# One set of weight buffers for two phases of a two-layer encoder, and the second phase's first inputs in the first phase's list schedule

## The chip, the cores and the metric

The kernel runs on one core of a Trainium2 chip. The core has five instruction queues that run side by side and meet at semaphores: TensorE (PE, matrix multiplication, with its weight loads shown as PEld), VectorE (DVE), ScalarE (ACT), GpSimd (POOL) and SyncE (SP), which here issues every DMA. The metric is device time in microseconds for one launch; smaller is better.

## What is computed

The reference is a trunk of two layers on 512 positions with 1024 channels (batch 1). Layer 0 mixes with a recurrent part (RWKV-7, both directions) and a long convolution (Hyena, by Fourier transform); layer 1 mixes with neighbourhood attention. Each layer then has a gated feed-forward part with a width-3 convolution, and a gated embedding.

```python
for i in range(DEPTH):                       # DEPTH = 2
    if i % 2 == 0:
        z = rmsnorm(h, mix_norm[j]) @ mix_w_in[j]
        y_a = rwkv7_bidir(z[..., :RWKV_COLS], ...)     # a scan in time, per head a 64 x 64 state
        y_b = hyena_bidir(z[..., RWKV_COLS:], ...)     # irfft(rfft(s) * rfft(kernel))
        h = h + jnp.concatenate([y_a, y_b], axis=-1) @ mix_w_out[j]
    else:
        z = rmsnorm(h, na_norm[j]) @ na_w_qkv[j]
        h = h + neighbourhood_attention(z, ...) @ na_w_out[j]
    h = h + conv_ffn(h, ffn_norm[i], ffn_w_up[i], ffn_conv_w[i], ffn_conv_b[i], ffn_w_down[i])
    h = h + per_layer_embedding(h, p[i], ple_norm[i], ple_w_gate[i], ple_w_proj[i])
```

## The kernel before

Activations lie channel-major: `self.h` is eight tiles of 128 channels x 512 positions. Every float32 product is made of three matmuls on parts of reduced precision: an operand x is split into a high part `xh` and the rest `xl`, a weight into `whi` and `wlo` (or two `wp` tiles), and `mm3` (line 647) adds xh·whi, xh·wlo and xl·whi in PSUM. So each weight costs a load, a cast (high part, on ACT) and a subtraction (rest).

**First phase: layer 0's mixer, `mixer0` (line 783).** Its instructions are not issued as they are written. A `Plan` (line 227) records them as steps, `both_mixers` (line 924) gives each piece of work a group (`part`, line 917), and `schedule` (line 408) makes a list schedule: at each point the engine that can start first takes the ready step with the highest rank. A rank is 1000 times the group's number from the table `ORDER` (line 830), or from `MOVED` where that names the group, plus the step's longest path to the end (`ranks`, line 393). With `DRAG` 0 (line 233) every step of a group has at least the rank of the group's first step. `in_order` (line 852) then holds each engine to this order.

The groups: `x` and `norm` load and split the input; `low`, `z` 0 to 3 and `hyena` 0 to 3 project it with `mix_w_in`, one 128-column block after another (`columns`, line 1036: 24 matmuls of 128x512); `prep` makes the recurrent part's operands for each pair of heads and direction; `inverse` inverts the triangular blocks of pair m (a long chain of short DVE instructions and small matmuls); `scan` m (line 1372) goes through 8 chunks in time, each with three steps in which PE waits for ACT or DVE (tiles `uv`, `r0`, `dg`, `x`); `out` m finishes the pair. `filters`, `fparts`, `kf`, `signals`, `ab`, `back` are the convolution by Fourier tables (`in_dft_f`, `in_dft_i`); `emb` 0 and 1 multiply the layers' embeddings by `proj` and store the result to DRAM (`pj_d`). `early`, `mid` and `last` are the output projection of the two halves of h, in three sets of inputs (`mix_w_out_a`, `mix_w_out_b`); `last` needs the last pair's output.

Weights of this phase are taken by `item` (line 882) in halves of 512 columns: a raw tile from `wr` (3 buffers), two split tiles from `wp` (12 buffers); the cast is ACT's, the subtraction POOL's. Parts that are kept longer go to slabs (`sl`, 39 buffers), the phase's common tiles.

**Second phase.** With the first phase's pools closed, `run` (line 744) opens `wraw`, `whi`, `wlo` (3 buffers of 1024 columns each), and the rest is issued as written: `ffn(0)`, `ple(0)`, `mixer1`, `ffn(1)`, `ple(1)`. `ffn` (line 1656) begins with `norm` (line 693): eight splits of h into `xh`, `xl` scaled by the gain, eight squares on ACT, seven additions on POOL. `gemm` (line 661) then goes through the up-weights in chunks of two input tiles (24 matmuls) and makes the row sums of the squares (`sums`) as a matmul after the second chunk.

Of the kernel before, what the change touches and what calls it, by code (L numbers as in the profile page):

```python
# [19 lines left out]
P = 128  # L20
# [206 lines left out]
class Plan:  # L227
# [5 lines left out]
    DRAG, SMALL = 0.0, 3  # L233
# [359 lines left out]
class Kern:  # L593
# [67 lines left out]
    def gemm(self, wname, g, k0, k1, xs, evac, then=(), rounds=1):  # L661
# [10 lines left out]
        for kc in range(k0, k1, KC):  # L672
# [3 lines left out]
            chunks.append((kc, nk, *self.load_split(src, nk * W)))  # L676
# [16 lines left out]
    def norm(self, h, gain):  # L693
# [44 lines left out]
    def gemm_pools(self, st, bufs, side):  # L738
        self.wraw = self.pool(st, "wraw", bufs=bufs, side="right")
        self.whi = self.pool(st, "whi", bufs=bufs, side=side)  # L740
        self.wlo = self.pool(st, "wlo", bufs=bufs, side=side)


    def run(self):
        nc, a = self.nc, self.a
        with ExitStack() as top:
# [19 lines left out]
            with ExitStack() as st:  # L766
                self.gemm_pools(st, 3, "left")
# [15 lines left out]
    def mixer0(self):  # L783
# [16 lines left out]
        with ExitStack() as st:  # L800
# [6 lines left out]
            self.rstd0 = self.h[4]  # L807
# [6 lines left out]
            self.wr = self.pool(st, "wr", bufs=3, side="right")  # L814
            self.wp = self.pool(st, "wp", bufs=self.PARTS, side="right")
# [12 lines left out]
    SLABS, PARTS = 39, 12  # L828

    ORDER = dict(start=180, x=200, low=198.5, norm=120, filters=75, scan=100, inverse=84, prep=80, z=79, out=60,  # L830
                 hyena=50, fparts=40, kf=67, signals=70, ab=58, back=46, early=30, emb=25, consts=86, mid=72,
                 last=99, norm1=98, next=55)


    MOVED = {("back", 0): 57.5, ("back", 2): 35.5, ("early", 0): 28.5, ("hyena", 2): 26.5, ("kf", 0, 1): 30.5,
             ("mid", 1): 32.5, ("scan", 0): 86.5, ("early", 1): 36.5}

    def order(self, group):
# [7 lines left out]
        if name in ("prep", "z"):  # L846
            n = [5 * n[0]]
# [34 lines left out]
    def item(self, held=False):  # L882

        t = []
        srcs = self.sources.popleft()
        for y in srcs:
            t.append(self.wr.tile([P, S], F32, name="wr"))
            self.nc.sync.dma_start(out=t[-1], in_=y)
        r = [self.slab(F32R) if held else self.wp.tile([P, S], F32R, name="wp") for _ in range(2)]
        self.nc.scalar.copy(r[0], t[0])  # L890
        if len(t) == 1:
            self.tt(r[1], t[0], r[0].bitcast(F32), ALU.subtract, self.nc.gpsimd)
        else:
            self.nc.gpsimd.tensor_copy(out=r[1], in_=t[1])
        return r

    def weights(self, name, g):
# [6 lines left out]
        for k in range(0, K // P, KC):  # L904
            nk = min(KC, K // P - k)
            src = self.a[name][base + k * P * W:base + (k + nk) * P * W].rearrange("(p a) -> p a", p=P)
            out += [(src[:, i:i + 512],) for i in range(0, nk * W, 512)]
        return out

    def table(self, name, fc, j):  # L910
        src = self.a[name][fc]
        return src[:, j * 1024:j * 1024 + 512], src[:, j * 1024 + 512:j * 1024 + 1024]
# [4 lines left out]
    def part(self, group, what, *args, sources=()):  # L917

        before, self.nc.group = self.nc.group, group
        self.sources = deque(sources) if sources else self.sources  # L920
# [3 lines left out]
    def both_mixers(self):  # L924
# [3 lines left out]
        self.sources = deque()  # L928
# [44 lines left out]
        where = (self.h[0:2], self.h[2:4], self.h[5:7], (self.h[7], self.slab()))  # L973
# [19 lines left out]
        for l in range(2):  # L993
            for g in range(2):
                for j in range(4):
                    what = [(a["pT"][l, k],) for k in range(2)] if (g, j) == (0, 0) else []
# [950 lines left out]
```

## Time and profile before

| | us |
|---|---|
| median of 3 runs | 1597.08 (1593.35 to 1598.9) |
| the profiled execution | 1602.47 |
| its span | 1600.7 |
| PE busy | 1531.0 (96%) |
| DVE busy | 973.9 (61%) |
| ACT busy | 718.8 (45%) |
| POOL busy | 341.0 (21%) |
| mean granted clock of TensorE | 0.974 |

The profile is of one execution. Busy time is the time in which an engine had an instruction running; idle time before an instruction is put down to what ended it (its releaser). Matmuls overlap, so their pace is the distance from start to start. The granted clock is a share of full speed: 1.00 is 2.4 GHz, 0.50 is 1.2 GHz, and a value between is a stretch with both.

### The profile page before, as it was taken

The page shows a single profiled execution, that of the slowest core. Times are in us where ns is not written, and L with a number is a line of the kernel's source. Part 1 is how long each engine was busy: PE and PEld are TensorE (multiplying, and loading weights), DVE is VectorE, ACT ScalarE, POOL GpSimd, SP SyncE. Part 2 cuts the span into 40 slices and gives each one's busy share as a digit, 9 for nine tenths or more (in the row PEclk, how much of TensorE's full clock was granted, in tenths as well). Part 3 has the DMA queues.
Part 4 walks back from the last instruction along what each step waited for, and adds up shares of the span by engine and source line. Part 5 has one row for each costly group of instructions (what it writes and reads, how often), then busy time and mean ns, then how long its engine had stood idle before and what let it go on. Part 6 is the DMA issues. An engine that isn't in the chain of part 4 may idle for free.

```text
span 1600.7 us, 24569 instructions
## 1 busy us (share of the span) xinstructions
PE 1531.0 (96%) x9520; PEld 1219.6 (76%) x9520; DVE 973.9 (61%) x1618; ACT 718.8 (45%) x1210; POOL 341.0 (21%) x296
## 2 busy tenths in 40 slices
PE   7999999979797999999999999999999999999998
PEld 6766777657585888888888878777678888888886
DVE  4875677775654477534674664565666665366655
ACT  5636455535344344313443554564554443144332
POOL 4654554433554000000001332011030000000020
PEclk9999999979898999999999999999999999999999
DMA  7456464766354323223243234224122332222431
GB/s 235 122 126 193 139 195 130 226 206 203 128 184 135 100 96 102 92 96 102 92 128 122 86 112 124 94 81 130 61 66 79 105 105 93 93 88 97 160 104 66
DMA packets 114583, 195.97 MB, mean 122 GB/s; under 512 B 27537, under 2 KB 57105, under 8 KB 114466
## 3 DMA queue, kind: packets, MB, share of 16 engines
q1 hardware_dynamic: 114466, 194.40, 38.4%
q8 instruction: 75, 1.23, 0.3%
q14 instruction: 42, 0.34, 0.1%
HBM read 163.95 MB, written 28.84 MB: 120 GB/s over the span
## 4 chain that ended last, share of the span: by engine, by line
PE 84%; DVE 5%; DMA 4%; ACT 3%; SPq 2%; issue 1%; POOL 1%; POOLq 0%; DVEq 0%; ACTq 0%
PE g L627 61%; PE b L590 19%; DVE w L590 3%; SPq L590 2%; PE m L627 2%; PE s L627 1%; ACT w L590 1%; PE m L1892 1%; DMA wr<-in_mix_w_in 1%; POOL w L590 1%; DMA wr<-in_dft_f 0%; POOL nacc L633 0%; ACT oh L641 0%; DVE u L633 0%; DVE uv L590 0%
## 5 line engine op out<-in xcount | busy, mean ns | idle before, releaser
L633 DVE TENSOR_TENSOR wlo<-wraw,whi 128x1024 fp32r<-128x1024 f32 x180 | 227.8, 1267 | 322.5 <-ACT whi L641 317.7
L641 ACT CAST whi<-wraw 128x1024 fp32r<-128x1024 f32 x180 | 188.2, 1046 | 406.7 <-PE g L627 398.5
L627 PE MATMUL g<-xh,whi 128*128 128x512 f32 x832 | 326.8, 393 | 8.9 <-ACT whi L641 8.9
L627 PE MATMUL g<-xh,wlo 128*128 128x512 f32 x832 | 325.3, 391 | 1.0 <-DVE wlo L633 1.0
L627 PE MATMUL g<-xl,whi 128*128 128x512 f32 x832 | 324.9, 391 | 0.0
L627 PEld LDWEIGHTS g<-xh,whi 128*128 128x128 f32 x832 | 157.0, 189 | 43.0 <-ACT whi L641 9.3
L627 PEld LDWEIGHTS g<-xh,wlo 128*128 128x128 f32 x832 | 156.8, 188 | 34.7 <-DVE wlo L633 1.7
L627 PEld LDWEIGHTS g<-xl,whi 128*128 128x128 f32 x832 | 157.1, 189 | 32.3
L633 POOL TENSOR_TENSOR nacc<-nsq 128x512 f32<-128x512 f32 x5 | 8.8, 1767 | 760.5 <-PE g L627 639.6
L590 PE MATMUL b<-xh,wp 128*128 128x512 f32 x432 | 151.0, 423 | 10.5 <-ACT wp L590 10.2
L627 PE MATMUL g<-hh,whi 128*128 128x512 f32 x352 | 137.2, 390 | 0.0
L627 PE MATMUL g<-hl,whi 128*128 128x512 f32 x352 | 137.0, 389 | 0.0
L627 PE MATMUL g<-hh,wlo 128*128 128x512 f32 x352 | 136.9, 389 | 0.0
L630 DVE SCALAR_TENSOR_TENSOR c<-u,prm,c 128x511 f32<-128x511 f32 x176 | 126.3, 746 | 6.4 <-ACT c L636 5.9
L590 PEld LDWEIGHTS b<-xh,wp 128*128 128x128 f32 x432 | 83.2, 197 | 36.2 <-ACT wp L590 12.0
L636 ACT ACTIVATE c<-u,prm 128x512 f32<-128x512 f32 x88 | 70.3, 816 | 70.7 <-DVE u L633 70.7
L590 POOL TENSOR_TENSOR wp<-wr,wp 128x512 fp32r<-128x512 f32 x62 | 82.5, 1343 | 50.0 <-ACT wp L590 41.0
L590 POOL TENSOR_TENSOR w<-w 128x256 f32<-128x256 f32 (+2 forms) x69 | 75.7, 1115 | 74.2 <-ACT w L590 57.1
L590 PE MATMUL b<-xl,wp 128*128 128x512 f32 x216 | 89.0, 418 | 0.0
L633 DVE TENSOR_TENSOR u<-g,rstd 128x512 f32<-128x512 f32 x104 | 71.3, 686 | 11.6 <-PE g L627 10.8
L627 PE MATMUL g<-wlo,xh 128*128 128x512 f32 x192 | 77.2, 402 | 0.0
L627 PE MATMUL g<-whi,xh 128*128 128x512 f32 x192 | 77.1, 401 | 0.0
(181 smaller groups left out, 2601.4 us busy)
## 6 DMA issues: line engine op xcount, KB each, us to landing
wraw<-in_up SPq DMA_DIRECT2D x88, 512.0 KB, 3.5
wraw<-in_down SPq DMA_DIRECT2D x44, 512.0 KB, 3.5
wr<-in_mix_w_in SPq DMA_DIRECT2D x52, 256.0 KB, 3.7
wraw<-in_na_w_qkv SPq DMA_DIRECT2D x24, 512.0 KB, 3.5
x<-ch_d SPq DMA_DIRECT2D x16, 640.0 KB, 5.1
ch_d<-w SPq DMA_DIRECT2D x64, 128.0 KB, 2.3
wraw<-in_gate SPq DMA_DIRECT2D x16, 512.0 KB, 3.5
tab<-in_rpb SPq DMA_DIRECT2D x8, 768.0 KB, 4.2
```

The source lines that it names most:

```text
L590: getattr(e, method)(*args, **kw)
L627: return self.nc.tensor.matmul(out, lhsT, rhs, start=start, stop=stop, skip_group_check=not group)
L630: return self.nc.vector.scalar_tensor_tensor(out=out, in0=in0, scalar=scalar, in1=in1, op0=op0, op1=op1)
L633: return (eng or self.nc.vector).tensor_tensor(out=out, in0=in0, in1=in1, op=op)
L636: return self.nc.scalar.activation(out=out, in_=in_, func=func, **kw)
L641: self.nc.scalar.copy(h, src)
L1892: nc.tensor.transpose(pst[:, i], sc[:, i // 2, (i % 2) * P:(i % 2 + 1) * P], ident)
```

## The change

Six things change together.

- The second phase's `wraw`, `whi`, `wlo` are opened before the first phase and serve both. `wr` and `wp` are gone. `item` now loads 1024 columns at once (512 KB) and splits them in two halves; a Fourier table's high and low halves share one buffer.
- The first phase's slabs go from 39 to 37, the scan's `uv` tiles from 4 to 3; `rstd0` has a tile of its own, which frees `h[4]` of that use.
- A new group `norm1` makes the eight splits `xh`, `xl` for the feed-forward part, and a new group `next` loads and splits its first two weight pieces. `ffn(0)` takes both over: `norm` skips the splits, `gemm` takes the pieces from `self.ready`.
- In `ffn(0)` the squares are added on DVE instead of POOL.
- `DRAG` becomes 1e9, so that within a group each step has the rank of its own longest path.
- `ORDER` and `MOVED` have new numbers. Their effect is shown below by the order of the instructions.

```diff
-    DRAG, SMALL = 0.0, 3
+    DRAG, SMALL = 1000000000.0, 3
...
-            chunks.append((kc, nk, *self.load_split(src, nk * W)))
+            chunks.append((kc, nk, *(ready.popleft() if ready else self.load_split(src, nk * W))))
...
-    def norm(self, h, gain):
+    def norm(self, h, gain, xs=()):
...
-        xs = []
+        adder = nc.vector if xs else nc.gpsimd
+        xs = list(xs)
         acc = None
-        for k in range(KT):
+        for k in range(len(xs), KT):
...
-                self.tt(new, acc, sq, ALU.add, nc.gpsimd)
+                self.tt(new, acc, sq, ALU.add, adder)
...
+            self.whi = self.pool(top, "whi", bufs=3)
+            self.wlo = self.pool(top, "wlo", bufs=3)
             ph = self.pool(top, "ph", side="right")
+            self.wraw = self.pool(top, "wraw", bufs=3, side="right")
...
-            self.wr = self.pool(st, "wr", bufs=3, side="right")
-            self.wp = self.pool(st, "wp", bufs=self.PARTS, side="right")
...
-    SLABS, PARTS = 39, 12
+    SLABS = 37
...
-                 hyena=50, fparts=40, kf=67, signals=70, ab=58, back=46, early=30, emb=25, consts=86, mid=72,
+                 hyena=50, fparts=43, kf=48, signals=70, ab=44, back=59, early=30, emb=41, consts=76, mid=60,
...
-    MOVED = {("back", 0): 57.5, ("back", 2): 35.5, ("early", 0): 28.5, ("hyena", 2): 26.5, ("kf", 0, 1): 30.5,
+    MOVED = {("ab", 0): 36.5, ("early", 0): 32.5, ("emb", 1): 58.5, ("hyena", 0): 41.5, ("kf", 1, 1): 84.5,
...
+        if not self.halves:
+            src, apart = self.sources.popleft()
+            n = src.shape[1]
+            raw = self.wraw.tile([P, 1024], F32, name="wraw")
+            nc.sync.dma_start(out=raw[:, :n], in_=src)
+            if not held:
+                hi = self.whi.tile([P, 1024], F32R, name="whi")
+                lo = hi[:, 512:] if apart else self.wlo.tile([P, 1024], F32R, name="wlo")
+                self.chunk = hi, lo
+            for i in range(0, 512 if apart else n, 512):
+                c = slice(i, i + 512)
+                self.halves.append((raw[:, c], raw[:, 512:] if apart else None,
+                                    *([self.slab(F32R), self.slab(F32R)] if held else [hi[:, c], lo[:, c]])))
+        x, y, h, l = self.halves.popleft()
+        nc.scalar.copy(h, x)
...
+        self.part("norm1", self.norm1)
+        nc.gates["next"] = [self.ys[LATE[4]][0]]
+        self.part("next", self.first_weights, sources=self.weights("up0", 0)[:2])
...
+    def norm1(self):
+
+        self.normed = []
+        for k in range(KT):
+            x = (self.px.tile([P, S], F32R, name=f"xh{k}"), self.px.tile([P, S], F32R, name=f"xl{k}"))
+            self.split(*x, self.h[k], scale=self.par("ffn_norm", k))
+            self.normed.append(x)
+    def first_weights(self):
+
+        self.ready = deque()
+        while self.sources:
+            for _ in range(2):
+                self.item()
+            self.ready.append(self.chunk)
...
-            uv = uvs[hf] = rb.tile([P, 2, 2, 4, 64], F32, name="uv", bufs=4)
+            uv = uvs[hf] = rb.tile([P, 2, 2, 4, 64], F32, name="uv", bufs=3)
...
-            xs, rstd, then = self.norm(self.h, lambda k: self.par("ffn_norm", l * 8 + k))
+            xs, rstd, then = self.norm(self.h, lambda k: self.par("ffn_norm", l * 8 + k),
+                                       self.normed if l == 0 else ())
```

Three places in the instruction order. The first is SP's queue at the end of the first phase; L655 (both kernels) is the load of the second phase's `gemm`, `in_up` are the feed-forward part's up-weights. Before:

```order
L590 DMA wr<-in_mix_w_out_b 128x512
L590 DMA pj_d_133<-w 128x512
L590 DMA pj_d_134<-w 128x512
...
L590 DMA pj_d_140<-w 128x512
L655 DMA wraw<-in_up 128x1024 x24
```

After:

```order
L590 DMA wraw<-in_mix_w_out_b 128x1024 x2
L590 DMA wraw<-in_up 128x1024
L590 DMA wraw<-in_mix_w_out_b 128x1024 x2
L590 DMA wraw<-in_up 128x1024
L590 DMA wraw<-in_mix_w_out_b 128x512 x2
L655 DMA wraw<-in_up 128x1024 x22
```

The first two of the 24 loads have moved ahead of the last projection weights, and the eight stores of the embedding have moved away from there.

The second is ACT's queue at the same place: `h` tiles, their scaled casts `xh`, squares `nsq`, and the casts of weights, of which whi_6112 (before) and whi_1199 (after) are the up-weights' first. Before:

```order
L636 ACTIVATE xh7_6070<-h7_80,prm_59 128x512
L636 ACTIVATE nsq_6074<-h0_73 128x512
L636 ACTIVATE nsq_6076<-h1_74 128x512
L636 ACTIVATE nsq_6080<-h2_75 128x512
L636 ACTIVATE nsq_6084<-h3_76 128x512
L636 ACTIVATE nsq_6088<-h4_77 128x512
L641 CAST whi_6112<-wraw_6110 128x1024
L636 ACTIVATE nsq_6092<-h5_78 128x512
```

After:

```order
L590 CAST whi_1199<-wraw_1198 128x512 x2
...
L590 CAST whi_1202<-wraw_1201 128x512 x2
L590 CAST whi_1169<-wraw_1168 128x512
L590 CAST whi_1176<-wraw_1175 128x512
L590 ACTIVATE xh0_1182<-h0_82,prm_59 128x512
L590 ACTIVATE xh1_1184<-h1_83,prm_59 128x512
L590 ACTIVATE xh2_1186<-h2_84,prm_59 128x512
L641 CAST whi_6012<-wraw_6010 128x1024
L590 ACTIVATE xh3_1188<-h3_85,prm_59 128x512
```

The casts of the first two up-weight pieces have moved from behind the squares to ahead of the last projection's own pieces (whi_1169, whi_1176).

The third is PE's queue in the fourth scan at its fourth chunk (`uv`, `r0`, `dg`, `x` are the scan's tiles; the chain goes from `uv<-` with `w` to `r0` to `uv` with `x`). Before:

```order
L590 MATMUL b_786<-uv_770,dg_785 64x64 x4
L590 MATMUL b_775<-x_772,uv_770 64x64 x4
L590 MATMUL b_786<-r0_787,w_760 64x64 x2
L590 MATMUL b_786<-r0_787,w_761 64x64 x2
L590 MATMUL b_786<-uv_770,x_772 64x64 x4
L590 MATMUL b_775<-x_772,uv_770 64x64 x4
L590 MATMUL b_793<-uv_773,w_706 64x64
```

After:

```order
L590 MATMUL b_748<-uv_732,dg_747 64x64 x4
L590 MATMUL b_970<-w_955,whi_968 128x512
L590 MATMUL b_970<-w_958,whi_968 128x512
L590 MATMUL b_962<-w_949,whi_961 128x512
L590 MATMUL b_962<-w_952,whi_961 128x512
L590 MATMUL b_970<-w_959,whi_968 128x512
L590 MATMUL b_970<-w_958,whi_968 128x512
L590 MATMUL b_963<-w_955,whi_961 128x512
L590 MATMUL b_963<-w_956,whi_961 128x512
L590 MATMUL b_737<-x_734,uv_732 64x64 x4
L590 MATMUL b_748<-r0_749,w_722 64x64 x2
```

Eight matmuls of group `ab` now stand between two steps of the chain that followed each other before.

## Rows read from the trace of the kernel before

**Rows 1.** Windows: length; busy time of PE, PEld, DVE, ACT, POOL; granted clock; DMA
```profile
7.78:504.94 497.16, 459.48 (x4504) 348.26 (x4504) 330.39 (x616) 245.64 (x521) 245.35 (x226) 0.94 0.56 169
7.78:296.00 288.22, 275.49 (x2860) 207.94 (x2860) 204.56 (x398) 151.48 (x312) 152.31 (x150) 0.96 0.56 164
296.00:370.00 74.00, 60.07 (x634) 43.82 (x634) 53.32 (x108) 38.31 (x89) 36.90 (x32) 0.84 0.72 216
370.00:440.00 70.00, 60.71 (x698) 44.94 (x696) 41.33 (x64) 29.63 (x76) 26.81 (x23) 0.90 0.49 160
522.33:1600.70 1078.37, 1063.93 (x5000) 865.84 (x4998) 633.86 (x990) 459.73 (x670) 83.51 (x49) 1.00 0.30 99
```
**Rows 2.** Timeline of PE at the seam: start, duration, instruction [idle before, releaser]
```profile
502.91 2.03 PE L590 MATMUL b<-w,wp 128*128 128x512 f32 x8
513.81 0.80 PE L627 MATMUL g<-xh,whi 128*128 128x512 f32 x1 [8.87 <-ACT whi L641]
...
516.00 0.79 PE L627 MATMUL g<-xh,wlo 128*128 128x512 f32 x1 [0.97 <-DVE wlo L633]
...
520.43 0.63 PE L627 MATMUL g<-xh,whi 128*128 128x512 f32 x1
520.85 0.63 PE L627 MATMUL g<-xl,whi 128*128 128x512 f32 x1
...
522.33 0.40 PE L627 MATMUL g<-xh,wlo 128*128 128x512 f32 x1
522.56 0.40 PE L627 MATMUL g<-xh,whi 128*128 128x512 f32 x1
```
**Rows 3.** Timeline of SP's DMA issues at the seam
```profile
499.32 6.95 SPq L590 DMA_DIRECT2D pj_d<-w  x8
506.38 20.20 SPq L655 DMA_DIRECT2D wraw<-in_up  x7
```
**Rows 4.** Timeline of ACT at the seam
```profile
512.19 0.63 ACT L636 ACTIVATE nsq<-h 128x512 f32<-128x512 f32 x1 [0.85 <-POOL nacc L633]
512.73 1.03 ACT L641 CAST whi<-wraw 128x1024 fp32r<-128x1024 f32 x1
```
**Rows 5.** Waits of PE from 296 to 440 us: sum, times, longest
```profile
PE b L590 <- ACT uv L590: 11.8, 11, 2.1
PE b L590 <- DVE uv L590: 4.6, 5, 1.8
...
PE b L590 <- ACT r L590: 0.7, 1, 0.7
```
**Rows 6.** Waits of PE from 8 to 296 us, the longest group
```profile
PE b L590 <- ACT wp L590: 10.2, 4, 7.8
```
**Rows 7.** Groups of DVE instructions: busy, mean ns (440 to 520, then 0 to 440)
```profile
L590 DVE TENSOR_TENSOR h<-b,h 128x512 f32<-128x512 f32 x16 | 9.9, 682 | 25.3 <-PE b L590 25.3
L630 DVE SCALAR_TENSOR_TENSOR xl<-h,prm,xh 128x512 fp32r<-128x512 f32 x8 | 5.6, 745 | 1.3 <-ACT xh L636 1.3
...
L590 DVE TENSOR_TENSOR w<-w 128x512 f32<-128x512 f32 x5 | 5.4, 1113 | 1.5 <-ACT w L590 1.5
...
L590 DVE TENSOR_TENSOR w<-w 128x512 f32<-128x512 f32 x36 | 26.6, 774 | 4.1 <-DMA w<-nd 1.9 <-ACT w L590 1.5
...
L590 DVE SCALAR_TENSOR_TENSOR xl<-h,prm,xh 128x512 fp32r<-128x512 f32 x8 | 7.3, 970 | 4.8 <-ACT xh L590 4.8
```
**Rows 8.** Timeline of PE in the third scan
```profile
343.15 0.45 PE L590 MATMUL b<-uv,w 128*64 128x64 f32 x8 [2.12 <-ACT uv L590]
...
353.12 2.93 PE L590 MATMUL b<-w,wp 128*128 128x512 f32 x6 [1.77 <-ACT wp L590]
```
**Rows 9.** Timeline of PE, the filler of layer 1's embedding
```profile
490.65 8.97 PE L590 MATMUL b<-w,wp 128*128 128x512 f32 x38
```
**Rows 10.** The tile `wp`: duration ns least/median/greatest, first and last start
```profile
L590 POOL TENSOR_TENSOR wp<-wr,wp x62: 1269/1292/1717, 7.8 to 487.0; 128x512 fp32r<-128x512 f32 x62
```

More of the change, by code (lines that the diff above doesn't have):

```diff
@@ L826, in mixer0 @@
             self.in_order(start)
-    SLABS, PARTS = 39, 12
-    ORDER = dict(start=180, x=200, low=198.5, norm=120, filters=75, scan=100, inverse=84, prep=80, z=79, out=60,
-                 hyena=50, fparts=40, kf=67, signals=70, ab=58, back=46, early=30, emb=25, consts=86, mid=72,
-                 last=99, norm1=98, next=55)
-    MOVED = {("back", 0): 57.5, ("back", 2): 35.5, ("early", 0): 28.5, ("hyena", 2): 26.5, ("kf", 0, 1): 30.5,
-             ("mid", 1): 32.5, ("scan", 0): 86.5, ("early", 1): 36.5}
+    SLABS = 37
+    ORDER = dict(start=180, x=200, low=198.5, norm=120, filters=75, scan=100, inverse=84, prep=80, z=77, out=60,
+                 hyena=50, fparts=43, kf=48, signals=70, ab=44, back=59, early=30, emb=41, consts=76, mid=60,
+                 last=99, norm1=98, next=40)
+    MOVED = {("ab", 0): 36.5, ("early", 0): 32.5, ("emb", 1): 58.5, ("hyena", 0): 41.5, ("kf", 1, 1): 84.5,
+             ("z", 0): 79.5}
     def order(self, group):
@@ L882, in item @@
     def item(self, held=False):
[L884 to L892, printed above, removed]
-        else:
-            self.nc.gpsimd.tensor_copy(out=r[1], in_=t[1])
-        return r
+        nc = self.nc
+        if not self.halves:
[13 more added lines that the diff above has]
+        nc.scalar.copy(h, x)
+        if y is None:
+            self.tt(l, x, h.bitcast(F32), ALU.subtract, nc.gpsimd)
+        else:
+            nc.gpsimd.tensor_copy(out=l, in_=y)
+        return h, l
     def weights(self, name, g):
@@ L905, in weights @@
             nk = min(KC, K // P - k)
-            src = self.a[name][base + k * P * W:base + (k + nk) * P * W].rearrange("(p a) -> p a", p=P)
-            out += [(src[:, i:i + 512],) for i in range(0, nk * W, 512)]
+            out.append((self.a[name][base + k * P * W:base + (k + nk) * P * W].rearrange("(p a) -> p a", p=P), False))
         return out
     def table(self, name, fc, j):
-        src = self.a[name][fc]
-        return src[:, j * 1024:j * 1024 + 512], src[:, j * 1024 + 512:j * 1024 + 1024]
+        return self.a[name][fc][:, j * 1024:j * 1024 + 1024], True
     def put(self, out, in_):
@@ L919, in part @@
         before, self.nc.group = self.nc.group, group
-        self.sources = deque(sources) if sources else self.sources
+        if sources:
+            self.sources, self.halves = deque(sources), deque()
         what(*args)
@@ L927, in both_mixers @@
         self.ys = [None] * KT
[L928 removed]
+        self.sources, self.halves = deque(), deque()
         self.xs, self.bon, self.m1, self.zt, self.emb = [], {}, {}, {}, {}
@@ L972, in both_mixers @@
         kf = [[[], []], [[], []]]
-        where = (self.h[0:2], self.h[2:4], self.h[5:7], (self.h[7], self.slab()))
+        where = [self.h[i:i + 2] for i in range(0, KT, 2)]
         for j in range(2):
@@ L995, in both_mixers @@
                 for j in range(4):
-                    what = [(a["pT"][l, k],) for k in range(2)] if (g, j) == (0, 0) else []
+                    what = [(a["pT"][l, k], False) for k in range(2)] if (g, j) == (0, 0) else []
                     self.part(("emb", l), self.embedding, l, g, j,
@@ L1004, in both_mixers @@
             nc.gates["mid", g] = self.ys[7][:1]
-            self.part(("mid", g), self.out_late, g, LATE[:4], sources=late[g][:4])
+            self.part(("mid", g), self.out_late, g, LATE[:4], sources=late[g][:2])
         for g in range(2):
             nc.gates["last", g] = [self.ys[LATE[4]][0], ("mid", g)]
-            self.part(("last", g), self.out_late, g, LATE[4:], sources=late[g][4:])
+            self.part(("last", g), self.out_late, g, LATE[4:], sources=late[g][2:])
+        self.part("norm1", self.norm1)
+        nc.gates["next"] = [self.ys[LATE[4]][0]]
+        self.part("next", self.first_weights, sources=self.weights("up0", 0)[:2])
     def norm0(self, xin):
@@ L1024, in norm0, with rms @@
                 self.tt(acc, acc, sq, ALU.add)
+        self.rms(acc, self.rstd0)
+    def norm1(self):
[10 more added lines that the diff above has]
+            self.ready.append(self.chunk)
+    def rms(self, acc, out):
+        nc = self.nc
         ps = self.bank(4)
@@ L1033, in norm0 @@
         nc.scalar.copy(ex.rearrange("p (t x) -> p t x", t=4), r[:, 0:4].unsqueeze(2).to_broadcast([P, 4, P]))
-        nc.scalar.copy(self.rstd0, self.back(ex))
+        nc.scalar.copy(out, self.back(ex))
     def columns(self, out):
@@ L1688, in ffn @@
                         self.gemm(f"up{l}", i * 2 + half, 0, KT, xs, lambda j, ps, h=half, e=evac: e(j, ps, h),
-                                  then if i == half == 0 else ())
+                                  then if i == half == 0 else (), self.ready)
                 k0 = i0 * 4
```

13 lines of the change are left out of this document (4 added, 9 removed).

## The prediction

> **What bounds the kernel now.** I read the page's first part (TensorE, PE, is the busiest engine by far), then the windows by stage, the timeline of PE and of the two queues that feed it at the seam between the stages, and the waits of PE in the first phase. The question is where PE waits and where it runs at half its clock. The windows give three stages [rows 1]. From 522.33 us to the end PE is busy 1063.93 of 1078.37 us with a granted clock of 1.00, and the change touches nothing there but names of buffers. The first phase (list schedule, up to 504.94) is busy 459.48 of 497.16 us at a mean clock of 0.94: 37.7 us of waiting, plus the slow clock. Between them lies the seam.
>
> The seam is read from PE's timeline [rows 2]. The last group of the first phase starts at 502.91 and takes 2.03, so it ends at 504.94. The first matmul of the feed-forward part starts at 513.81 after 8.87 idle, the third waits 0.97 more, and then they follow each other every 0.43 us (520.43 to 520.85), where the steady pace is 0.23 (522.33 to 522.56): the lower level of the clock, 1.2 instead of 2.4 GHz, until about 522. Seventeen matmuls were started between 513.81 and 522.33; at the steady pace they are 17 x 0.23 = 3.9 us. The seam therefore costs 522.33 - 504.94 - 3.9 = 13.5 us. Its cause is seen on two queues: SP issues the first up-weights at 506.38, behind eight stores of `pj_d` that wait for the last embedding copies [rows 3]; and ACT reaches the cast of these weights at 512.73, behind a square that waits for an addition on POOL [rows 4].
>
> Inside the first phase the waits are uneven: PE is idle for 13.9 + 9.3 = 23.2 us between 296 and 440 [rows 1], and 11.8 + 4.6 + 0.7 = 17.1 us of it, in 17 waits, are for `uv` and `r0` of the recurrent scan [rows 5]. From 7.78 to 296 it is idle for 288.22 - 275.49 = 12.7 us [rows 1], and the rest, some 2 us, lies after 440.
>
> **The change part by part.** The sum is made against the profiled execution, 1602.47 us (span 1600.7 and 1.8 around it); that is 5.4 above the median of the runs, 1597.08, and I take 5.4 off at the end.
>
> *The seam.* In the order of the changed kernel two loads of up-weights stand between the loads of the late output projection, their casts on ACT and subtractions on POOL are done before the last projection group, and `pj_d` stores no longer stand at the end. The inputs of the first two chunks (tiles 0 to 3) are split on ACT and DVE while PE still has 26 matmuls (6 us) of `mid` 1. So the first feed-forward matmul can follow directly, and PE keeps its clock: the 13.5 us go. What is late next is the sum of squares, now on DVE. The matmuls that use it stand behind 48 matmuls (48 x 0.23 = 11.0 us). DVE must do, from the last accumulator group of `mid` 1 on (about 0.9 us before the seam), six additions into h at 0.682, four `xl` at 0.745 and seven additions of squares, whose nearest row is the addition of two SBUF tiles at 0.774 [rows 7]: 4.1 + 3.0 + 5.4 = 12.5, less 0.9 is 11.6 us, against 11.0. With the hops to ACT I put 1 us of waiting there. Term: **-12.5 us**; bounds -13.5 (the additions hide) and -9.6 (see rival 3). The sums on POOL which this replaces cost nothing on PE's path, since PE asked for them later; nor does ACT (eight squares, eight casts) last longer than DVE.
>
> *The scan.* Each of the four scans has 23 steps in which PE waits for ACT or DVE; the planner puts matmuls of other groups between them. I counted in the order the steps with no such matmul ahead: before 0, 0, 9 and 10 for the four scans, after 0, 0, 5 and 7. The 17.1 us of waits in 17 places fit the 19 bare steps: 0.9 us each [rows 5]; one is seen at 343.15, 2.12 us [rows 8]. Seven fewer: **-6.3 us**, bounds 0 (what fills them is late itself, as the 1.77 us wait of a filler for its weights at 353.12 [rows 8]) and -6.3.
>
> *The clock in the same stretch.* Granted 0.84 over 74 us and 0.90 over 70 us [rows 1]: (0.16 x 74) + (0.10 x 70) = 18.8 us of half-rate loss. In proportion to the bare steps (7 of 19) that is 6.9 us at most, nothing at least, since idle time at the low level loses nothing. The stretch keeps twelve bare steps, so I take less than half: **-3 us**.
>
> *Fillers.* The embedding of layer 1, 48 matmuls at 0.236 (8.97 us for 38 of them [rows 9]), moves from the last 15 us to ahead of the first scan. Its work is the same in both places, at the end it covered nothing that PE had to wait for, and ahead of the scan it can fill some of the waits before 296 [rows 1]: bounds 0 and -5 (less than half of these waits, since most lie elsewhere), taken **-1**. That it leaves the end costs nothing while the splits of the late projection keep up (rival 4).
>
> *Buffers.* Weights come in pieces of 1024 columns with three raw and three split buffers, instead of pieces of 512 with three and twelve halves. Three pairs hold the same six halves, but a pair comes free only when both halves are used; slabs fall from 39 to 37 and `uv` from 4 to 3. The trace shows no such wait; the nearest are PE's waits for a split piece: three of 0.8 us on average before 296 (10.2 us in four, less 7.8 for the first matmul [rows 6]) and the 1.77 at 353.12 [rows 8]. Bounds: 0, and 24 columns x 0.8 = 19 us. Since the three buffers prefetch two columns and a column has 24 matmuls (5.5 us), I take the near end: **+2 us**. At the start the first piece is twice as large; the second half of a column then comes earlier than before, so I leave it at nothing, bounds ±0.8 (one such wait).
>
> Sum: -12.5 - 6.3 - 3 - 1 + 2 = -20.8 us: 1581.7 against the profiled execution, **1576 us** against the median.
>
> **The rivals.**
>
> 1. *Only the seam.* The new order moves the waits of the first phase about and gains nothing net. For it: fillers are finite, the same work is only placed elsewhere. Against: fewer bare steps. 1602.5 - 12.5 - 5.4 = 1585 us.
>
> 2. *All of it.* The clock stays up where steps are filled and the early waits go: -12.5 - 6.3 - 6.9 - 5 = -30.7: 1566 us. For it: slow-clock windows sit where the bare steps are.
>
> 3. *The sums of squares take the seam's place.* If DVE runs in its slower form (six at 0.682, four at 0.97 and seven at 1.113, the highest means of like instructions elsewhere in the phase [rows 7]), it needs 15.8 - 0.9 = 14.9 us against 11.0: PE waits 3.9, the seam gives -9.6: 1579 us.
>
> 4. *POOL becomes the bound at the end.* From the first late-projection piece on POOL has 14 subtractions, four of them new, while PE has 120 matmuls (27.6 us). At the median of 1.292 that is 18.1 us and hidden, at the slowest of 1.717 [rows 10] 24.0 us: some 6 us more, and since the last pieces are wanted before PE's last matmul, up to that much is seen: 1582 us. The Trainium skill (SBUF — State Buffer, section "SBUF: two separate sides") says that DVE and GpSimd take their shared pair of ports as a lock for a whole instruction, if DVE reads two SBUF inputs. By that rule each of the 14 could wait for a whole `xl` of 0.745, some 10 us in all, an estimate that would give 1586 us; the spread from 1.292 to 1.717 [rows 10] is as much as the trace bears out, since additions into h read PSUM and only one SBUF tile.
>
> 5. *The gap stays.* The two early pieces hold two of the three split buffers, so the last projection group has one, and waits move there instead: the 8.87 us come back. 1585 us. Against: the order has 12 matmuls of `last` 0 before `last` 1 needs the buffer.
>
> 6. *Slower.* The ring of three whole pieces starves PE in the first phase: place, the 24 columns of `z` and `hyena`; price, the longest wait for a piece, 1.77 us [rows 8], in each: 42.5 us instead of +2, so 1602.5 - 22.8 + 42.5 - 5.4 = 1617 us. It decides from 13 columns on (22.8 / 1.77). For it: DMA latencies vary most in this phase. Against: the same prefetch depth as before. Half-way, at 8 to 15 such waits, the result is within 0.3%.
>
> **How the numbers follow.** About 0.3% (4.8 us) is what a measurement of this kernel can tell from no change. Chances: forecast 0.39 (1570 to 1582), rival 1 0.20, rival 2 0.17, rival 3 0.07, rival 4 0.05, rival 5 0.03, the half-way case of rival 6 0.05, rival 6 0.04. All but the last two are faster by over 0.3%: 0.91; within 0.05; slower 0.04. The range reaches from below rival 2 (1560) to past rivals 1 and 5 (1591); it leaves out the last two cases and the fringes.
>
> **What would show it.** In the changed profile: the first feed-forward matmul within 1 us of the last one of the first phase, at the 0.23 pace; a wait of at most 2 us on the additions of squares some 11 us later; waits for `uv` and `r0` near 11 us in 12 places in the second half of the phase; the first phase ending near 496 instead of 505; the stretch behind the seam 1078 us long as before. I am wrong if PE waits for pieces of `mix_w_in` in many places (rival 6), if the late projection waits for POOL (rival 4), or if bare steps in the second scan pair are paid for by longer single waits (rival 1).

## The result and the profile after

| | before | after |
|---|---|---|
| median, us | 1596.91 (20 runs, 1593.28 to 1603.13) | 1588.4 (20 runs, 1582.92 to 1594.39) |
| span of the profiled execution, us | 1600.7 | 1592.6 |
| first phase on PE, first to last matmul, us | 497.16 | 498.53 |
| PE idle in it, us | 37.7 | 37.8 |
| what the seam costs, us | 13.5 | 4.3 |
| mean granted clock | 0.974 | 0.977 |

The ratio of the times is 0.9941, with a 95% interval of 0.9928 to 0.9955: faster by 0.6%, some 9 us. The sign was forecast and the range (1560 to 1591) held the time, but the forecast, 1576, promised more than twice the gain. Both profiled executions lie about 6 us above the median of their kernel, so they may be set against each other.

The windows of the changed kernel, with the same columns as [rows 1]: length; busy time of PE, PEld, DVE, ACT, POOL; granted clock; DMA.

```profile
8.87:507.40 498.53, 460.72 (x4505) 349.45 (x4505) 329.07 (x609) 244.46 (x522) 250.28 (x230) 0.94 0.58 175
8.87:296.00 287.13, 275.14 (x2568) 205.86 (x2570) 191.24 (x367) 144.46 (x300) 153.92 (x146) 0.95 0.56 167
296.00:370.00 74.00, 62.87 (x868) 46.52 (x863) 56.10 (x119) 39.28 (x96) 31.80 (x31) 0.88 0.59 167
370.00:440.00 70.00, 58.72 (x686) 44.33 (x684) 40.74 (x65) 34.28 (x78) 28.54 (x25) 0.94 0.67 218
440.00:507.40 67.40, 63.99 (x393) 52.74 (x393) 40.98 (x60) 26.44 (x50) 36.02 (x29) 0.96 0.53 179
517.14:1592.60 1075.46, 1060.77 (x4993) 863.16 (x4991) 635.64 (x993) 460.38 (x671) 83.55 (x49) 1.00 0.30 99
```

Nothing was won in the first phase. PE is idle for 498.53 - 460.72 = 37.8 us of it, as before. It starts 1.1 us later, and its end has moved from 504.94 to 507.40. The stretch behind 440 us, which [rows 1] do not show by itself, was before:

```profile
440.00:504.94 64.94, 63.22 (x316) 51.56 (x316) 31.19 (x48) 26.22 (x45) 29.33 (x24) 1.00 0.45 145
```

The last row of the windows after begins at the 25th matmul of the feed-forward part; from the same matmul on, the kernel before needs 1076.75 us, so the rest is as long as it was within about 1 us.

The gain lies at the seam, which [rows 2] showed before. PE's timeline after:

```profile
507.17 0.39 PE L590 MATMUL b<-xh,w 128*128 128x512 f32 x1
507.40 0.39 PE L627 MATMUL g<-xh,whi 128*128 128x512 f32 x1
...
509.89 0.39 PE L627 MATMUL g<-xh,wlo 128*128 128x512 f32 x1
512.70 0.50 PE L627 MATMUL g<-xh,whi 128*128 128x512 f32 x1 [2.42 <-DVE h L590]
...
513.75 0.63 PE L627 MATMUL g<-xl,whi 128*128 128x512 f32 x1
514.18 0.63 PE L627 MATMUL g<-xh,wlo 128*128 128x512 f32 x1
...
517.14 0.40 PE L627 MATMUL g<-xh,whi 128*128 128x512 f32 x1
...
522.62 0.94 PE L627 MATMUL m<-con,nacc 128*128 128x1 f32 x8
```

The first feed-forward matmul (507.40) follows the last one of the first phase at the steady pace, as forecast. After twelve matmuls PE waits 2.42 us for an addition into `h` on DVE, which no step of the prediction had. About 1 us after it starts again its pace falls to the lower level of the clock, from 0.23 to 0.43 (513.75 to 514.18), until 517.14. The sums of squares (`nacc`, 522.62), where I had put 1 us of waiting, are there in time. From 507.40 to 522.62 PE issues 48 matmuls, 10.9 us at 0.2275; the seam costs 15.2 - 10.9 = 4.3 us.

DVE's timeline in the same microseconds shows what the addition stood behind (start, duration, instruction [idle before, releaser]):

```profile
506.68 1.42 DVE L590 TENSOR_TENSOR h<-b,h 128x512 f32<-128x512 f32 x2 [1.96 <-PE b L590]
508.36 0.75 DVE L590 SCALAR_TENSOR_TENSOR xl<-h,prm,xh 128x512 fp32r<-128x512 f32 x1 [0.26 <-ACT xh L590]
509.49 0.75 DVE L590 SCALAR_TENSOR_TENSOR xl<-h,prm,xh 128x512 fp32r<-128x512 f32 x1 [0.38 <-ACT xh L590]
510.16 0.69 DVE L590 TENSOR_TENSOR h<-b,h 128x512 f32<-128x512 f32 x1
510.76 0.68 DVE L633 TENSOR_TENSOR nacc<-nsq 128x512 f32<-128x512 f32 x1
511.36 1.28 DVE L590 TENSOR_TENSOR h<-b,h 128x512 f32<-128x512 f32 x2
```

All six additions could run from 507.6 on, when PE's last matmul was done, but two `xl` and a sum of squares stand ahead of the fifth. It ends at 512.6, and PE goes on at 512.70. Why PE needs it is not in the profile but in the built program: the third accumulator of the feed-forward part (`g`) has bank 4 of PSUM (the memory that matmuls add up in), the bank of the accumulator that this addition reads. The Trainium skill (Perfetto Trace Analysis, section "Matmuls") says that independent groups of matmuls should go round the PSUM banks, so that one group's evacuation lies beside the next one's matmuls. They do so here (the four `g` have banks 2, 5, 4 and 3), and the trace shows the limit of it: the 2.42 us are an evacuation (the reading of an accumulator out of its bank) that came late because of other work ahead of it on DVE.

In the first phase the waits have changed hands. PE's waits from 296 to 440 us, to be read against [rows 5] (sum, times, longest), and then those for `uv` from 440 us to the seam, where the kernel before has none, since its fourth scan is over by 440:

```profile
PE b L590 <- ACT whi L590: 7.9, 4, 4.9
PE b L590 <- ACT uv L590: 4.7, 5, 2.0
PE b L590 <- DVE uv L590: 2.8, 2, 2.4
```

```profile
PE b L590 <- ACT uv L590: 2.9, 3, 1.8
```

The scan's own waits fell from 17.1 us in 17 places to 4.7 + 2.8 + 2.9 = 10.4 in 10. PE's idle time did not fall with them. By the windows, from 296 us to the end of the phase, it is 11.1 + 11.3 + 3.4 = 25.8 us, where it was 13.9 + 9.3 + 1.7 = 24.9. Most of what came in their place lies between the third and the fourth scan. There PE waited 1.77 us [rows 8] and 0.56 before, 2.3 in all, and waits 2.07 + 1.50 + 1.19 + 4.90 = 9.7 us now; the first fence is before, the second after:

```profile
357.94 3.05 PE L590 MATMUL b<-con,w 128*128 128x128 f32 x13 [0.56 <-DMA w<-s_d]
```

```profile
368.57 1.12 PE L590 MATMUL b<-w,con 128*128 128x512 f32 x2 [2.07 <-DVE w L590]
...
374.06 1.05 PE L590 MATMUL b<-con,w 128*128 128x2 f32 x8 [1.50 <-ACT w L590]
...
378.61 2.13 PE L590 MATMUL b<-w,whi 128*128 128x512 f32 x8 [1.19 <-ACT whi L590]
...
389.12 3.78 PE L590 MATMUL b<-w,whi 128*128 128x512 f32 x8 [4.90 <-ACT whi L590]
```

The matmuls that now fill the scans' steps are missing in the gap behind them: between its small matmuls (64x64 and 32x32, from 366.12 to 380.5) stood 30 of 128x512 before, and 8 stand there now (378.61, from 370.49 to 384.2). And those that come wait for their own weights (`whi`). Which of the two weighs more, no run separates.

### The profile page after: what moved, and what is told of

It reads as the page before. It is cut to its first block, busy times and chain, and to the rows that moved or that the text cites. A ratio compares the mean times of both kernels' runs of the same rounds, so it can differ in the third digit from the quotient of the medians.

```text
span 1592.6 us, 24430 instructions
## 1 busy us (share of the span) xinstructions
PE 1528.8 (96%) x9520; PEld 1218.2 (76%) x9520; DVE 976.3 (61%) x1623; ACT 715.9 (45%) x1210; POOL 334.4 (21%) x293
## 4 chain that ended last, share of the span: by engine, by line
PE 83%; DMA 4%; DVE 4%; ACT 2%; SPq 1%; issue 1%; POOL 1%; DVEq 0%; ACTq 0%; POOLq 0%
PE g L627 61%; PE b L590 18%; DVE w L590 2%; PE s L627 1%; PE m L627 1%; SPq L590 1%; DMA wraw<-in_proj 1%; PE m L1920 1%; DMA wraw<-in_dft_f 1%; DMA w<-kt_d 1%; ACT oh L641 0%; DVE u L633 0%; DVE ol L633 0%; PE m L1871 0%; POOL nacc L633 0%
## 5 line engine op out<-in xcount | busy, mean ns | idle before, releaser
L633 DVE TENSOR_TENSOR wlo<-wraw,whi 128x1024 fp32r<-128x1024 f32 x178 | 223.8, 1259 | 311.0 <-ACT whi L641 306.2
L590 PE MATMUL b<-xh,whi 128*128 128x512 f32 x216 | 91.5, 423 | 10.7 <-ACT whi L590 10.7
L590 POOL TENSOR_TENSOR wlo<-wraw,whi 128x512 fp32r<-128x512 f32 x66 | 88.4, 1361 | 60.7 <-ACT whi L590 51.4
L590 PE MATMUL b<-xh,wlo 128*128 128x512 f32 x216 | 91.0, 428 | 0.8 <-POOL wlo L590 0.6
L590 PE MATMUL b<-xl,whi 128*128 128x512 f32 x216 | 90.8, 421 | 0.0
L627 PEld LDWEIGHTS g<-hh,whi 128*128 128x128 f32 x352 | 66.1, 188 | 14.2 <-DVE u L633 0.5
```

The lines of the kernel that those rows point to most:

```text
L590: getattr(e, method)(*args, **kw)
L627: return self.nc.tensor.matmul(out, lhsT, rhs, start=start, stop=stop, skip_group_check=not group)
L633: return (eng or self.nc.vector).tensor_tensor(out=out, in0=in0, in1=in1, op=op)
```

## The experiments

All times are medians of 4 to 12 runs, with 9 to 17 runs of the kernel before beside them.

**Additions first.** One number:

```diff
-                 last=99, norm1=98, next=40)
+                 last=99, norm1=58, next=40)
```

> The changed kernel with one number changed: group norm1 gets rank 58 instead of 98, below mid 1, so that DVE makes the six last additions into h ahead of the xl of tiles 4 to 7. Theory (bank): the third accumulator of the feed-forward part lies in the PSUM bank of the sixth tile's mid accumulator, and PE's 2.42 us wait there lasts until DVE, busy with two xl and one sum of squares, has drained it; with the additions first the wait is at most 0.5 us, the pace stays 0.23, the sums of squares are still ready when the matmuls on them come, and the time falls by 3 to 4 us to about 1584.5. Rival (DVE is short of time as a whole): the wait moves to the sums of squares, 2 to 3 us about 11 us behind the seam, and the time stays at 1588.

Measured: 1583.05 us, ratio 0.9912 (0.9889 to 0.9934). By the ratios that is 4.6 us less than the changed kernel (0.9941) and 2.1 less than its second series further down (0.9925); the second difference lies within the intervals, so the repair is shown by the trace at the seam and not by the time. On PE, POOL and SP the order is the same as in the changed kernel, on DVE and ACT up to the seam too. DVE and then PE there:

```profile
491.91 3.34 DVE L590 TENSOR_TENSOR h<-b,h 128x512 f32<-128x512 f32 x5 [1.96 <-PE b L590]
495.24 0.69 DVE L633 TENSOR_TENSOR nacc<-nsq 128x512 f32<-128x512 f32 x1
...
496.45 2.73 DVE L590 SCALAR_TENSOR_TENSOR xl<-h,prm,xh 128x512 fp32r<-128x512 f32 x4
499.10 4.61 DVE L633 TENSOR_TENSOR nacc<-nacc,nsq 128x512 f32<-128x512 f32 x6
```

```profile
492.63 0.39 PE L627 MATMUL g<-xh,whi 128*128 128x512 f32 x1
...
495.35 0.44 PE L627 MATMUL g<-xh,whi 128*128 128x512 f32 x1
...
503.76 1.05 PE L627 MATMUL m<-con,nacc 128*128 128x1 f32 x8
```

Five additions now run in one piece (3.34 us), the thirteenth matmul of `g` (495.35) comes at the steady pace, and the pace never falls: 503.76 - 492.63 = 11.1 us for 48 matmuls, a seam of 0.2 us. The theory of the bank holds. DVE was not short of time; its order was wrong.

**Sums of squares on POOL.**

```diff
-        adder = nc.vector if xs else nc.gpsimd
+        adder = nc.gpsimd
```

> The changed kernel with the sums of squares on POOL again, all else as it is. Theory (bank): PE's wait at the seam falls only by the one sum of 0.6 us that stood ahead of the sixth tile's addition, from 2.4 to 1.8 us; POOL's seven sums at 1.7 to 1.9 each need some 13 us from the second square on and are wanted 13 us after it, so PE waits 0 to 3 us there: 1588 to 1590. Rival (DVE is short of time as a whole at the seam): the wait goes to nothing and the time falls by 3 to 4 us to 1584.

Measured: 1587.34 us, ratio 0.994 (0.9919 to 0.996): as the changed kernel. PE, then POOL:

```profile
504.12 0.77 PE L627 MATMUL g<-xh,whi 128*128 128x512 f32 x1 [1.94 <-DVE h L590]
...
514.00 0.95 PE L627 MATMUL m<-con,nacc 128*128 128x1 f32 x8
```

```profile
504.00 8.94 POOL L633 TENSOR_TENSOR nacc<-nacc,nsq 128x512 f32<-128x512 f32 x6 [0.74 <-ACT nsq L636]
```

The wait of 2.42 us falls to 1.94, about by the one sum that stood ahead, as the theory of the bank says. POOL's seven sums (the first at 501.95) end at 512.9, before PE asks for them. At the seam 514.00 - 499.29 - 10.9 = 3.8 us are lost. The move of the sums to DVE brought nothing and cost about 0.5 us there, too little to be seen in the time.

**No seam groups.**

```diff
-        self.part("norm1", self.norm1)
-        nc.gates["next"] = [self.ys[LATE[4]][0]]
-        self.part("next", self.first_weights, sources=self.weights("up0", 0)[:2])
+        self.normed, self.ready = (), deque()
```

> The changed kernel without the groups norm1 and next and with the sums of squares on POOL again: only the buffers, DRAG and the new order are left. Theory (the gain is all seam): the seam costs 13.5 us as before instead of 4.2, the first phase ends near 505 to 507, and the time is 1597, that of the kernel before. Rival (buffers and order gain, and the two new groups take it back inside the first phase): the first phase ends near 496 and the time is 1588 or less.

Measured: 1595.65 us, ratio 0.999 (0.9976 to 1.0004). Without the two groups the change is worth nothing that can be told from noise. The window of the end of the first phase, and PE at the seam:

```profile
440.00:506.96 66.96, 61.13 (x352) 49.30 (x352) 36.72 (x52) 24.35 (x44) 28.17 (x22) 0.97 0.51 173
```

```profile
506.56 0.40 PE L590 MATMUL b<-xh,wlo 128*128 128x512 f32 x1
511.27 0.76 PE L627 MATMUL g<-xh,whi 128*128 128x512 f32 x1 [4.31 <-DVE h L590]
...
517.64 0.40 PE L627 MATMUL g<-xh,whi 128*128 128x512 f32 x1
```

The seam itself is cheaper than before: the sixteenth matmul of `g` starts at 517.64, 517.64 - 506.79 - 15 x 0.228 = 7.4 us are lost instead of 13.5. The `pj_d` stores and a queue of squares no longer stand ahead of the weights, which are issued at 482.90 (506.38 before) and cast at 506.81 (512.73 before). What PE waits for, 4.31 us, is again an addition into `h`; in the built program it reads the bank of the first `g`. But from 440 us to the seam PE is idle for 5.8 us where it was 1.7 before. New order and buffers without the groups give with one hand and take with the other.

**Buffers alone, and order alone.** The first keeps the new buffers and takes back the old numbers of `ORDER` and `MOVED`, the step of `z` and `prep` (the factor of `n` in the diff), and `DRAG`, and leaves out the groups; the second is the kernel before with the new numbers.

```diff
-    DRAG, SMALL = 1000000000.0, 3
+    DRAG, SMALL = 0.0, 3
...
-            n = [2 * n[0]]
+            n = [5 * n[0]]
```

> The changed kernel's buffers (ring of three 1024-column pieces, 37 slabs, three uv) with the old numbers of the order, DRAG 0 and without norm1 and next. Theory (buffers cost): later start by 1.1, waits for split weights longer by 4 us: 1602. Rival (the new order, not the buffers, ate the gain of the scan): 1597, as before.

> The kernel before with its own buffers (halves of 512 columns, 12 split buffers, 39 slabs, four uv) and without the new groups; only ORDER, MOVED, the step of z and prep, and DRAG are the changed kernel's. Theory (the new ring ate the gain of the scan): waits for uv and r0 near 11 us, waits for split weights near 6 us beside the first, the first phase 7 to 9 us shorter than before, 1588. Rival (the new order only moves the waits, whatever the buffers): other waits grow by as much as those of the scan fall, 1597 within 3 us.

Measured: 1660.98 us, ratio 1.04 (1.0377 to 1.0423), and 1623 us, ratio 1.016 (1.0126 to 1.0194). Both theories and both rivals miss by far. In each, PE has one wait of some 20 us in the first set of the output projection (`early`; the loads of `mix_w_out_b` come only after it); the buffers' first, then the order's:

```profile
490.09 1.22 PE L590 MATMUL b<-xh,w 128*128 128x512 f32 x2 [21.90 <-POOL w L590]
```

```profile
471.08 1.22 PE L590 MATMUL b<-xh,w 128*128 128x512 f32 x2 [19.72 <-POOL w L590]
```

The numbers of an order belong to one set of buffers. Either half of the change by itself loses 26 or 64 us, and the two together lose nothing: the new numbers are what pays for the shared buffers, not a gain of their own. The buffers' loss is not for want of weight pieces: beside the first matmul PE waits 14.4 - 8.2 = 6.2 us for `whi` in that run, and 22.2 + 17.7 + 13.2 = 53 us for slabs (`w`). Its longest wait, 21.90 us, is for a subtraction on POOL that stands behind eight others (11.1 us, from 477.68). So neither half can be priced with the other taken away; the two runs leave open what the ring costs in the new order.

**Loads in halves.** First with the planner told of it, so that everything is planned anew:

```diff
-            nc.sync.dma_start(out=raw[:, :n], in_=src)
+            for i in range(0, n, 512):
+                nc.sync.dma_start(out=raw[:, i:i + 512], in_=src[:, i:i + 512])
```

> The changed kernel with each 1024-column weight load of the first phase issued as two DMAs of 512 columns, so that the first half's cast waits for its own half alone. Theory (whole pieces): PE's waits for split weights (10.3 us beside the first one of 8.87, where the kernel before had 6.4 beside 7.8) come from pieces that must land whole; the first matmul starts near 7.8, the waits fall to about 6.4, and the time falls by 4 to 5 us to about 1584. Rival (the DMA queues are full where these pieces land late, or the order sets the waits): only the start moves, by 1 us, and the time is 1587 or more, since SP has some 50 more issues of 0.4 us.

Measured: 1607.36 us, ratio 1.0068 (1.005 to 1.0087). The start came earlier (7.20), but the planner, given other steps, made another order, with a wait of 7.0 us for DVE's additions at the seam and one of 8.4 for `wlo` inside. As a test of the pieces it is void. Then with nothing replanned, the one load issued as two where it stood:

```diff
+                if kw.get("in_") is not None and s.bytes and tuple(kw["out"].shape) == (P, 1024):
+                    for i in (0, 512):
+                        c = slice(i, i + 512)
+                        e.dma_start(out=kw["out"][:, c], in_=kw["in_"][:, c])
+                    continue
                 getattr(e, method)(*args, **kw)
```

> The changed kernel with every instruction in its place; only each 1024-column load of the first phase is issued as two DMAs of 512 columns where the one stood, so nothing is replanned. Theory (whole pieces cost): the first matmul starts near 7.3 as with the half loads before, the casts of first halves start earlier, the waits for split weights beside the first fall from 10 to some 6 us, and the time falls by 4 to 5 us to about 1584. Rival (traffic on the DMA queues, not the piece, sets when weights land): only the start's 1 to 1.5 us, 1587; the 19 us of the half loads then came from the replanning.

Measured: 1581.2 us, ratio 0.9902 (0.9876 to 0.9928). To find the part of it, the first load alone, the other loads alone, and the changed kernel itself once more ran together:

> The changed kernel itself once more, beside the next two and with a profile of its own. Theory (the profile of the changed kernel was one from the slow end, and differs from that of the additions first by clock alone ahead of the seam): the median is 1586 to 1589 again; in the first 296 us the waits of PE are those of the first profile within 2 us, but the stretches at the low clock lie elsewhere or are fewer, so that the first phase ends up to 10 us earlier or as late. Rival (the two kernels differ in the first phase): it ends near 507 again with the clock low from 122 to 142.

> The changed kernel with only the very first weight load issued as two halves in place. Theory (the start is the smaller part of what the split in place gave): the first matmul starts some 0.5 us earlier and the time is 1587 to 1588. Rival (the start is all of it): 1581 to 1582.

> The changed kernel with all 1024-column loads of the first phase but the first one issued as two halves in place. Theory (whole pieces cost inside the phase): 1582 to 1583, most of what the full split gave. Rival (the start is all of it): 1587 to 1588.

Measured: 1585.68 us (ratio 0.9925, 0.9899 to 0.9952), 1584.03 (0.9919, 0.9891 to 0.9948) and 1584.59 (0.9919, 0.9889 to 0.9949). The parts can't be told from the whole kernel or from each other. What the traces bear is smaller than the expectation: beside the first one, PE's waits for `whi` are 9.8 and 7.8 us in the two profiles of the changed kernel, 6.5 with all loads split and 5.7 with all but the first. With all loads split the first matmul starts at 8.15, not at 7.3. Whole pieces cost 1 to 4 us of waiting; whether the full split gave 4 or 7 us stays open, and the 4, against the second series, lie within the intervals.

The second profile of the changed kernel tells more. Its windows, and its waits for `uv` from 296 to 440 us:

```profile
8.18:497.76 489.58, 450.84 (x4504) 341.99 (x4505) 329.42 (x610) 244.93 (x522) 251.13 (x230) 0.96 0.58 179
8.18:296.00 287.82, 273.77 (x2748) 205.59 (x2749) 200.49 (x381) 150.55 (x313) 159.55 (x152) 0.98 0.58 174
296.00:370.00 74.00, 61.57 (x823) 45.45 (x822) 57.06 (x123) 38.33 (x91) 31.51 (x30) 0.88 0.64 186
370.00:440.00 70.00, 59.41 (x614) 44.40 (x614) 38.65 (x61) 31.45 (x76) 28.46 (x25) 0.90 0.55 182
```

```profile
PE b L590 <- ACT uv L590: 7.9, 8, 1.9
PE b L590 <- DVE uv L590: 2.8, 2, 2.4
```

The same program ended its first phase at 497.76 instead of 507.40. PE's idle time is 38.7 us (37.8 in the first profile); its busy time, for the same matmuls, is 450.84 instead of 460.72. The 10 us are the clock, as the expectation had it; its median, 1585.68, lies just below the 1586 to 1589 expected. The rest agrees with the first profile: waits for `uv` of 7.9 + 2.8 = 10.7 us in 10 places, none behind 440, 9.6 us of waits between the third and the fourth scan, and at the seam the same 2.42 us for an addition into `h` and 4.3 in all. The stretch from 130 to 140 us, first profile and then second:

```profile
130.00:135.00 5.00, 5.00 (x66) 4.30 (x62) 1.82 (x3) 2.78 (x7) 1.65 (x1) 0.50 1.03 343
135.00:140.00 5.00, 5.00 (x72) 4.26 (x69) 0.00 (x0) 3.19 (x7) 0.28 (x1) 0.50 0.23 83
```

```profile
130.00:135.00 5.00, 3.21 (x13) 2.54 (x13) 0.00 (x0) 2.85 (x7) 0.00 (x0) 0.74 0.86 285
135.00:140.00 5.00, 5.00 (x23) 3.92 (x22) 2.77 (x8) 2.83 (x7) 2.93 (x3) 0.92 0.23 57
```

**Both repairs**, additions first and loads split in place:

> Additions first (norm1 at rank 58) together with loads split in place. If both work by themselves and on different places, their gains add: 1583 less what the split in place gives, 1579 by the theory of whole pieces, 1582 by its rival.

Measured: 1578.12 us, ratio 0.9886 (0.9859 to 0.9913), the fastest of all with the next one. It beats both kernels; the seam costs 0.2 us (48 matmuls from 493.64 to 504.77). The gains add about as expected.

**Loads ahead of a store**, on top of both:

```diff
+            store = [s for s in order if s.engine == "sync" and s.group == ("inverse", 3)
+                     and any(t.startswith("xd3") for t in s.touch)][0]
+            loads = [s for s in order if s.engine == "sync" and s.group == ("emb", 0)
+                     and any(t.startswith("wraw") for t in s.touch)][:2]
+            order = [s for s in order if s not in loads]
+            i = order.index(store)
+            order[i:i] = loads
             plan.write(order)
```

> Both repairs as before, and in SP's queue the loads of the embedding's inputs and of its first weights (pT, proj) stand ahead of the store xd of the fourth inversion instead of behind it; the order on the other engines is the same. Theory (a filler's own loads queue behind a store that waits): SP stands some 10 us at that store with free buffers behind it, so the 4.4 to 5.1 us that PE waits for the split weights of the embedding at the end of the third scan fall to 1 us or less, the clock falls less there, and the time is 1573 to 1575 where both repairs gave 1578. Rival (the DMA traffic there is the limit, or PE then waits elsewhere for the fourth scan's operands): the wait moves to the next waits of the same stretch, and the time stays at 1577 to 1579.

Measured: 1578.36 us, ratio 0.9878 (0.9857 to 0.9899): no change. PE, then SP's DMA issues:

```profile
376.04 3.78 PE L595 MATMUL b<-w,whi 128*128 128x512 f32 x8 [3.31 <-ACT whi L595]
```

```profile
342.80 0.80 SPq L593 DMA_DIRECT2D wraw<-in_proj  x2
...
365.15 2.59 SPq L593 DMA_DIRECT2D wraw<-in_proj  x2
```

I had moved the wrong load. The first piece of `proj` went ahead of the store (342.80; the store is at 349.24), but the long wait is for the second, which is issued where it was (365.15): 3.31 us at 376.04, 4.38 without the move. Just ahead of it PE now waits 1.45 us for a copy on ACT, where it waited 0.78. The rival came true; that the second load's place is the cause was not tried.

## Why the prediction was wrong

**The scan** was forecast at -6.3 us. This is the step that failed: the premise that a step of the scan which is filled costs PE no wait. The count itself came out: waits for `uv` and `r0` fell from 17.1 us in 17 places to 10.4 in 10 and, in the second profile, 10.7 in 10, where I had put 11 in 12. But PE's idle time from 296 us to the end of the phase went from 24.9 us to 25.8, and to 24.7 in the second profile, so the term is worth nothing. The 6.7 us came back between the third and the fourth scan, where PE waits 9.7 and 9.6 us instead of 2.3. The lower bound of the term said why it could come to nothing, "what fills them is late itself", and I took the far end without looking for the place that the fillers are taken from. The traces show where the waits went; whether they went there because the fillers are used up or because their weights come late stays open.

**The seam** was forecast at -12.5 us and gave -9.2. Its mechanism was right as far as it went: weights and inputs early, the first matmul at the old pace, nothing lost at 507.40. The term was mis-sized by what is late next. I named the sums of squares; it was the accumulators' banks. My sum of DVE's work (additions, `xl`, sums) had all the instructions, but it asked only when the last of them is done, not in which order they come and what PE wants first. The price was not 2.42 us but 4.3, since the clock fell 1 us after the stall; in the additions-first run there is no stall and no fall. Rival 3's end, -9.6, was met by luck, for another reason. The additions-first run shows the full term: with them the seam costs 0.2 us, a gain of 13.3.

**The clock in the same stretch**, -3, was about right. By [rows 1] 18.8 us were lost to the lower level, with none behind 440 us (1.00). After it 0.12 x 74 + 0.06 x 70 + 0.04 x 67.4 = 15.8 us are lost to the end of the phase, in the second profile 0.12 x 74 + 0.10 x 70 = 15.9 and none behind 440. But the clock before 296 us, which I left alone, moves by more from one execution to the next (0.95 and 0.98, 0.96 before), and took it back: over the whole phase PE's busy time rose by 1.2 us.

**The early filler**, -1, gave nothing that two profiles show: before 296 us PE is idle 12.0 and 14.1 us in the two profiles, 12.7 before.

**The buffers**, +2, come to 1.4 to 5 us as far as they are shown, nearer to the term than to the 19 or 42 us of the far cases. The start came later by 0.4 to 1.1 us (8.18, 8.87 against 7.78), which I had put at nothing, and whole pieces add 1 to 4 us of waits. No run prices the fewer slabs and `uv` tiles in the new order. What I had not seen is how the two parts hang together: the old order on the new buffers is 64 us slower, and not by rival 6's starving, since PE's waits for `whi` come to 6.2 us in that run.

**The rivals.** Rival 1 (only the seam, 1585 us) describes the first phase: waits moved about, nothing net. It had 0.20 and should have had more, since the argument for it, that fillers are finite and the same work is only placed elsewhere, was stronger than a count of bare steps. Rival 4 (POOL at the end) did not come: PE waits for POOL only 1.2 us in the whole first phase, and not at all behind 440 us. Rival 5 fell with the first matmul at 507.40.

The sum, from the profile before and the first one after: -9.2 at the seam; +0.9 of idle time from 296 us to the end of the phase and -0.7 ahead of 296; +1.1 at the start; +1.2 of the first phase's busy time, which is clock; -1.3 behind the seam. That is -8.0; the two spans (1600.7 and 1592.6) differ by 8.1.

## What to carry to other kernels

When a stage's inputs are moved ahead of a seam, list for the first matmuls behind it every resource that they take over, accumulators' banks too, and see that what frees them comes first on its engine; a sum of the work says nothing of that. A wait that is filled with other work is only gone if that work is not missed where it stood before and its own loads and casts are early: price both before counting the wait as saved, and measure a stretch to the end of the work, not to a fixed time. An order that was tuned for one set of buffers cost 26 and 64 us here when one was changed without the other, so neither is priced alone.

## What the runs showed of the hardware

One and the same program gave 498.5 and 489.6 us for its first phase with 37.8 and 38.7 us of idle time on PE. Four profiles with this very order on PE (the two of the changed kernel, additions first, sums on POOL) have 460.72, 450.84, 448.56 and 455.35 us of busy time for the same matmuls. In one of them the clock was at the lower level between 130 and 140 us although PE had no idle time there; in the next PE idled 1.8 us at that place and the clock was back at 0.92 behind it. A term of a few microseconds in such a phase can't be sized from the busy time of two profiles; PE's idle time, 35.5 to 38.7 us in the four, is steadier.

A stall of 2.42 us at the seam was followed, 1 us after its end, by 3.4 us at the lower level: 4.3 us in all with the pace lost. The second profile repeats it, and with the sums on POOL a stall of 1.94 us was followed by 3.5 us at the lower level.
